# The second product of the attention's scores, contracted over 128 rows instead of 64 or 66

## The chip, the cores and the metric

The kernel runs on one core of a Trainium2 chip. The metric is the device time in microseconds of one execution; the median of three runs is 3224.2 us (3222.32 to 3228.08).

The engines of a core work side by side and wait for each other through semaphores. TensorE (PE in the profile; its weight loads stand apart as PEld) multiplies: one operand of up to 128 x 128 is loaded, the other streams past it column by column, and the rows of both are what the product contracts over. VectorE (DVE) and ScalarE (ACT) work on tiles of up to 128 partitions, GpSimd (POOL) has little to do in this kernel, and SyncE (SP) issues most transfers. The results of TensorE lie in PSUM, eight banks of 128 x 512 float32.

## The reference

One inference step of a two-layer backbone for 128 context tokens and 512 latent tokens of width 1024. Each layer has a half-step feed-forward, three gated mixers side by side (a gated DeltaNet, a grouped-query attention, a linear recurrence) and another feed-forward, all in float32. The attention of the latent tokens, on which the change bears, reads 128 cached context keys and 512 latent keys in one softmax:

```python
def blocked_attention(q, k, v):
    ...
    def one_block(qblk):
        s = jnp.einsum('bqkgd,bskd->bkgqs', qblk, k, preferred_element_type=jnp.float32) * scale
        p = jax.nn.softmax(s, axis=-1).astype(v.dtype)
        return jnp.einsum('bkgqs,bskd->bqkgd', p, v)
```

There are 8 query heads and 2 key heads of width 64, so head `j` and head `j + 4` (for `j` from 0 to 3) belong to the two key heads.

## The kernel before

Tokens stand in columns (640 of them, the context first), features on the 128 partitions; a half of the tokens has 320 columns. TensorE multiplies in a rounded form of float32 (`fp32r`), and each float32 operand is split into a rounded part and the rest (`wh` and `wl` of a weight; `t_H` and `t_A` of the activations), so that a product with weights is three matmuls. The layers follow each other; in a layer the first feed-forward, the mixers, the merge and the second feed-forward. Instructions are emitted in the order of the Python code, with generators that lay steps of one part beside another (`beside`), and a scheduling layer then places them on each engine's queue. Every engine takes its queue in order.

The scores of the attention are split in the same way. For a key head `g`, `kk[g]` holds the rounded keys twice, in both halves of the partitions, and a query operand `q1` holds the rounded queries in one half and their remainder in the other: one product over 128 rows gives two of the three terms. The third term, rounded queries (`q2`, rows 0 to 63) with the remainder of the keys (`kl[g]`, rows 0 to 63), is a second product into the same bank. The scores are computed twice:

- `att_max` (L990): for a pair of heads, query tiles of 128 against halves of 320 keys, only to find each query's maximum. 16 pairs of products for each `j` (2 heads, 4 query tiles, 2 halves), each followed by a maximum on VectorE (L1010). The minus maximum, in two parts, is then written into rows 64 and 65 of `q2`, where `kl[g]` has ones. These are the products `acc<-t_A,t_H` of the profile: 128 x 320 the first, 64 x 320 the second.
- `att_pv` (L1027): key tiles of 128 against all 512 queries, transposed; the second product contracts over 66 rows and so subtracts the maximum. Then the exponential on ScalarE and the products with the values. These are `acc<-t_H,t_A`, 128 x 512 and 66 x 512.

`att` (L1076) runs `att_max(0)` alone, and then, beside the key tiles of each `att_pv(j)`, two steps of `att_max(j + 1)`; a step is two pairs. `beside` lays parts of the merge (`tg`, `wacc<-t_A,wh`) between. Both operands of a head lie in one slot of class H (8 buffers, tile `t_H`); PSUM has five banks for `acc`, of which `att_pv` keeps two for a whole `j`, and three for `wacc`.

The line numbers of helpers, not of the callers, stand in the profile: L174 is every matmul, L154 every ScalarE instruction, L157, L161 and L165 most of VectorE's.

Of the kernel before, what the change touches and what calls it, by code (L numbers as in the profile page):

```python
# [18 lines left out]
P = 128  # L19
# [13 lines left out]
# inverse square root: the seed's bits, the two constants of the first step, the factor left to whoever reads it  # L33
# [14 lines left out]
def spread(n, a, b):  # L48
    """n things over the steps a to b: how many beside each step"""
    return lambda i: (min(max(i + 1 - a, 0), b - a) * n) // (b - a) - (min(max(i - a, 0), b - a) * n) // (b - a)  # L50


# vectors of the next layer's modulation done beside a layer's last feed-forward
MOD2 = 3
# the steps of a feed-forward that its feature tiles lie beside: the first layer's first one, a layer's last, the next's first
STEPS1, STEPS2, STEPS3 = (4, 66), (10, 66), (4, 66)
# tiles over which the first half runs ahead: the first of a feed-forward, its last ones, the last of the mixers
HEAD, TAIL, TAIL_O = 2, 2, 3
# buffers of split weights
WB = 7  # L60
# key tiles whose probabilities are not split
PVF = (0, 2)
# PSUM banks kept for products with weights
WBANKS = 3
# order of the halves of the tokens: that without context tokens is the sooner normed
HO = (1, 0)
# gate tiles emitted behind each projection of the DeltaNet; those left for the attention
FILL = ((1, 1, 0, 1, 1, 1), 4)
# steps emitted behind each step of the DeltaNet's solve, its back part, the attention, the attention's front
# [3 lines left out]
class Slots:  # L73
    """SBUF slots of a few sizes, shared by all that fits them"""
# [28 lines left out]
class Trunk:  # L103
# [24 lines left out]
    # ------------------------------------------------------------- helpers  # L128
# [7 lines left out]
    def late(s, out, in_):  # L136
        """a load that does not run ahead of what precedes it on the scalar queue"""
        s.tc.keep_in_program_order(s.nc.scalar.dma_start(out=out, in_=in_))

    def pairs(s, n):  # L140
        """n views of [P, T], two to a slot; and the slots"""
        regs = [s.A(2 * T) for _ in range(n // 2)]
        return [regs[i // 2].v(2)[:, i % 2, :] for i in range(n)], regs
# [44 lines left out]
    # ------------------------------------------------------------- weights  # L188
    def prep(s, src, nk, m=P):
        """(hi, lo) of weights, four tiles of rows at a time"""  # L190
        nc = s.nc
        parts = []
        for k0 in range(0, nk, WK):
            n = min(WK, nk - k0)
            w = s.wp.tile([P, WK, P], F32, name="w", tag="w", bufs=3)
            wh = s.wp.tile([P, WK, P], F32R, name="wh", tag="wh", bufs=WB)
            wl = s.wp.tile([P, WK, P], F32R, name="wl", tag="wl", bufs=WB)
            nc.sync.dma_start(out=w[:, :n, :m], in_=src[:, k0:k0 + n, :])
            s.act(wh[:, :n, :m], w[:, :n, :m])
            s.tt(wl[:, :n, :m], w[:, :n, :m], wh[:, :n, :m].bitcast(F32), ALU.subtract)  # L200
            parts.append((wh, wl))
        return parts
# [31 lines left out]
    # ------------------------------------------------------------- modulation  # L234
# [25 lines left out]
    def start(s, mc):  # L260
        """the first norm, with the two modulation vectors that it takes"""
# [44 lines left out]
    def mod_cols(s, mc, j, f, pin=False):  # L306
        """feature tile f of modulation vector j; pin: not ahead of what precedes it on the vector engine"""
        nc = s.nc
        l, m = mc["l"], mc["m"]
        cs = s.cs  # L310
        q = j * KT + f
        w = s.wm[q % 2]
        nc.sync.dma_start(out=w, in_=s.a["wmod"][l, q])
        i = s.stt(s.jk.ap, w, 0.5, cs[:, 0, :], ALU.mult, ALU.mult, accum_out=m[:, 0, q:q + 1])
        if pin:
            s.tc.keep_in_program_order(i)
        s.stt(w, w, 0.5, cs[:, 1, :], ALU.mult, ALU.mult, accum_out=m[:, 1, q:q + 1])
# [16 lines left out]
    def mod_steps(s, n):  # L334
        """n more feature tiles of the modulation under way"""
# [10 lines left out]
    # ------------------------------------------------------------- norms  # L346
    def rstd(s, v, out):
        """RS * out = v ** -0.5: a seed from the bits, a quadratic and a cubic step"""
# [54 lines left out]
    # ------------------------------------------------------------- feed-forward  # L403
    @staticmethod
    def halves(n, first, last):
        """(tile, half) with the first half ahead over the first `first` and the last `last` tiles"""
# [5 lines left out]
    def ffn(s, wgu, wd, i, mods, done):  # L412
        """mods(step): feature tiles of a modulation to emit beside; done(o, h): after the last update of a tile's half"""
# [37 lines left out]
    # ------------------------------------------------------------- mixers: shared pieces  # L451
    PADW = 646

    def conv_in(s, w):
        """a projection in padded columns; steps: each half"""
# [12 lines left out]
    def conv(s, xp, taps, bias=None):  # L468
        """centred depthwise convolution of width 4"""
# [11 lines left out]
    def head_rstd(s, xs, scale):  # L481
        """RS * r = (scale * (sum of squares over each 64 rows) + EPS) ** -0.5 for xs of [P, T], heads on partitions;
        returns what spreads r over the rows again: (tile, half) -> [P, H] in PSUM"""
# [21 lines left out]
    def log1p(s, e, n):  # L505
        """log(1 + e), 0 <= e <= 1, for small [P, n]; returns a region"""
# [13 lines left out]
    # ------------------------------------------------------------- gated DeltaNet  # L520
    def dn_front(s):
# [3 lines left out]
        # gates per token: beta and the log decay  # L525
# [3 lines left out]
        # k, q, v: convolution, silu, l2 norm  # L529
# [28 lines left out]
        # token-major k and v; k k^T and k q^T within chunks  # L558
# [33 lines left out]
    def dn_gates(s, baf):  # L592
        """beta, the log decays' running sums and what comes of them"""
# [21 lines left out]
        # running sums within a chunk, per direction; columns (t, d, h)  # L615
# [11 lines left out]
        # rows of gc, spread over the partitions by way of DRAM  # L627
# [22 lines left out]
    def dn_solve(s):  # L650
        """minus the inverses of the diagonal blocks of 32, one system to a partition"""
# [34 lines left out]
    def dn_join(s):  # L686
        """the blocks off the diagonal: minus the inverses of the 64 x 64 systems, transposed, in place"""
# [32 lines left out]
    def dn_back(s):  # L720
        """chunk by chunk, the directions side by side; rows of keys are (chunk of the token tile, dk)"""
# [22 lines left out]
        for i in range(NT):  # L744
            for d in range(2):
# [44 lines left out]
                # states; that ahead of a tile's first chunk is set by the tile before, but for the two starts  # L790
# [32 lines left out]
    def dn_gate(s):  # L823
        """2 silu(z), parked"""
# [11 lines left out]
    def dn_out(s):  # L836
        """per-head norm and silu(z) gate; leaves (hi, lo) of the branch's output"""
# [15 lines left out]
    # ------------------------------------------------------------- attention  # L853
    def att_front(s):
# [40 lines left out]
        # values, token-major  # L895
# [22 lines left out]
        # [v0 | 1 | v1 | low part of v0 | 0 | low part of v1] per key tile: the cache, then the latents  # L918
# [5 lines left out]
        # whole, for the key tiles that take float32 products  # L924
# [15 lines left out]
        for g in range(2):  # L940
# [6 lines left out]
            s.act(s.kl[g][64:66, :], s.ones[64:66, 0:1].to_broadcast([2, T]))  # L947
# [42 lines left out]
    def att_max(s, j, qs):  # L990
        """operands and row maxima for heads j and j + 4, into qs; a step: 128 queries of one head"""
# [3 lines left out]
        for g in range(2):  # L995
# [3 lines left out]
            q1, q2 = reg.r[:, :TL], reg.r[:, TL:2 * TL]  # L999
            s.act(q1[r], src)  # L1000
            s.act(q2[0:64], src)
            s.tt(q1[ro], src, q1[r].bitcast(F32), ALU.subtract)
            for qt in range(4):
                c = slice(qt * P, qt * P + P)
                for h in range(2):
                    ps = s.bank()
                    s.mm(ps[:, :H], q1[:, c], s.kk[g][:, s.hs(h)], True, False)
                    s.mm(ps[:, :H], q2[0:64, c], s.kl[g][0:64, s.hs(h)], False, True)
# [4 lines left out]
        # rows 64 and 65 of the second operand: minus the maximum, in two parts  # L1013
# [13 lines left out]
    def att_pv(s, j, qs):  # L1027
# [4 lines left out]
        for kt in range(NT):  # L1032
            pr = []
            c = slice(kt * P, kt * P + P)
            for g in range(2):
                st = s.bank()
                s.mm(st, s.kk[g][:, c], qs[g][1], True, False)
                s.mm(st, s.kl[g][0:66, c], qs[g][2][0:66], False, True)
# [62 lines left out]
    # ------------------------------------------------------------- RG-LRU  # L1101
    def lru(s):
# [5 lines left out]
        # kappa / 4 = -2 softplus(-lam)  # L1108
# [15 lines left out]
        for j in range(2):  # L1124
# [11 lines left out]
            for d in range(2):  # L1136
# [7 lines left out]
                # tau = tanh(log_a / 2); a = (1 + tau) / (1 - tau); sqrt(1 - a^2) = 2 sqrt(-tau) / (1 - tau)  # L1144
                s.act(y, tr, AF.Exp, scale=small.ap[:, 12 + i4:13 + i4], bias=small.ap[:, 12 + i4:13 + i4])
                s.act(tr, tr, AF.Tanh, scale=kq[:, i4:i4 + 1], bias=kq[:, i4:i4 + 1])
                # 1 / (1 - tau) = (1 + a) / 2; a Newton step
# [21 lines left out]
            # gelu (tanh form) of the y projection  # L1169
# [19 lines left out]
    # ------------------------------------------------------------- merge  # L1189
# [4 lines left out]
    def gates(s, n):  # L1194
        """tanh of half the gates' logits for n more of their tiles, parked"""
# [25 lines left out]
    @staticmethod  # L1221
    def beside(main, fill, n):
        """main's steps, with n[i % len(n)] steps of fill behind step i"""
        for i, _ in enumerate(main):
            for _ in range(n[i % len(n)]):
                next(fill, None)

    @staticmethod
    def both(*gs):
        """steps of several, in turn"""  # L1230
# [8 lines left out]
    def merge_first(s):  # L1239
        """the DeltaNet's and the RG-LRU's part of the merge"""  # L1240
# [66 lines left out]
    # ------------------------------------------------------------- the whole  # L1307
# [9 lines left out]
    def ahead_mix(s, l):  # L1317
        """the first weights of the mixers, ahead of the norm"""
        return lambda: [s.prep(s.a["wba"][l], KT, 16), s.prep(s.a["win"][l, 0], KT)]

    def ahead_ffn(s, wgu):
        """the first weights of a feed-forward"""
# [51 lines left out]
def _layout(i):  # L1374
# [11 lines left out]
    # columns of w_in by tile  # L1386
# [11 lines left out]
    # small parameters per partition  # L1398
# [17 lines left out]
    # (layer, direction, dk, head, dv)  # L1416
# [8 lines left out]
    # constants of the shapes  # L1425
# [51 lines left out]
```

## Time and profile before

| | before |
|---|---|
| timed runs, median (lowest to highest) | 3224.2 us (3222.32 to 3228.08) |
| profiled execution, its span (the page gives no other time of it) | 3222.9 us |
| what lies between the span and the median of the runs | 1.3 us |
| TensorE busy with matmuls, share of the span | 99% |
| VectorE, ScalarE, GpSimd busy | 61%, 36%, 0% |
| mean granted clock of TensorE | 0.990 |

The span is one profiled execution, from its first instruction to its last. "Busy" of an engine counts instructions under way, and since matmuls overlap, a busy TensorE isn't a TensorE at its peak; what a matmul costs is seen in the distance of one start from the next. "Idle before" of a group is the time in which the engine stood still just before its instructions, with what ended it; "issue" there means that nothing the profile shows was waited for.

### The profile page before, as it was taken

To read this page: it belongs to the slowest core of one execution; us is meant where nothing else is said; L and a number is where in the kernel's file an instruction comes from. 1 tells how busy PE (TensorE), PEld (TensorE's weight loads), DVE (VectorE), ACT (ScalarE), POOL (GpSimd) and SP (SyncE) were. 2 spreads that over 40 slices of the span, in tenths; PEclk is the share of its full clock that TensorE was granted. 3 is DMA by queue.
4 is the path that set the end of the run, shared out by engine and by line. 5 is a ranking of instruction groups with operands and counts; after the bars stand their busy time and mean duration, and the time that the engine had idled before them with its cause. 6 is when DMAs were issued, how large, how long until landed. Compare 5 with 4: busy or idle time off the path is not lost.

```text
span 3222.9 us, 54120 instructions
## 1 busy us (share of the span) xinstructions
PE 3176.3 (99%) x21446; PEld 2978.3 (92%) x21446; DVE 1981.2 (61%) x4040; ACT 1159.8 (36%) x2288; POOL 3.8 (0%) x6
## 2 busy tenths in 40 slices
PE   8999999999999999999999999999999999999999
PEld 5999998998976899999999999989889669999999
DVE  5677677667656774555566666685685576633332
ACT  4222324346434443222233222253563343432221
POOL 0000000000000000000000000000000000000000
PEclk9999999999989999999999999999999899999999
DMA  5444442454311422333324444434532124222222
GB/s 218 134 147 168 144 155 89 134 163 119 111 56 54 136 84 99 113 117 99 115 76 138 141 148 133 130 103 144 162 112 81 49 64 140 73 77 77 76 71 81
DMA packets 261466, 364.87 MB, mean 113 GB/s; under 512 B 97708, under 2 KB 144636, under 8 KB 260476
## 3 DMA queue, kind: packets, MB, share of 16 engines
q1 hardware_dynamic: 252572, 340.66, 33.6%
q10 hardware_dynamic: 8640, 20.76, 1.8%
q8 instruction: 168, 2.75, 0.3%
q14 instruction: 86, 0.70, 0.1%
HBM read 325.37 MB, written 35.96 MB: 112 GB/s over the span
## 4 chain that ended last, share of the span: by engine, by line
PE 92%; DVE 4%; ACT 2%; DMA 1%; issue 1%; SPq 1%; ACTq 0%; DVEq 0%
PE wacc L174 49%; PE acc L174 43%; ACT t_A L154 1%; DVE tn L165 1%; DVE t_H L165 1%; SPq L696 0%; DVE wl L157 0%; DMA w<-in_wgu 0%; ACT t_W L154 0%; ACT t_B L154 0%; DVE t_A L157 0%; DVE t L165 0%; DVE t_A L165 0%; DMA gd<-tg 0%; ACT t_H L154 0%
## 5 line engine op out<-in xcount | busy, mean ns | idle before, releaser
L174 PE MATMUL wacc<-t_H,wh 128*128 128x320 f32 (+1 forms) x5568 | 1259.7, 312 | 18.7 <-ACT t_H L154 8.5
L174 PEld LDWEIGHTS wacc<-t_H,wh 128*128 128x128 f32 (+1 forms) x5568 | 932.3, 188 | 42.6 <-ACT t_H L154 11.8
L174 PE MATMUL wacc<-t_H,wl 128*128 128x320 f32 (+1 forms) x2784 | 863.4, 311 | 2.3 <-DVE wl L157 2.3
L154 ACT ACTIVATE wh<-w 128x512 fp32r<-128x512 f32 (+2 forms) x796 | 485.7, 612 | 848.1 <-PE wacc L174 626.3
L157 DVE TENSOR_TENSOR wl<-w,wh 128x512 fp32r<-128x512 f32 (+2 forms) x796 | 527.8, 665 | 329.0 <-ACT wh L154 322.0
L174 PE MATMUL acc<-t_H,wh 128*128 128x320 f32 x2816 | 626.3, 308 | 0.0
L174 PEld LDWEIGHTS wacc<-t_H,wl 128*128 128x128 f32 (+1 forms) x2784 | 522.6, 188 | 11.1 <-issue 5.6
L174 PE MATMUL wacc<-t_A,wh 128*128 128x320 f32 x2048 | 471.8, 313 | 5.3 <-DVE tg L165 4.4
L174 PEld LDWEIGHTS acc<-t_H,wh 128*128 128x128 f32 x2816 | 471.7, 188 | 0.8 <-ACT wh L154 0.2
L174 PE MATMUL acc<-t_H,wl 128*128 128x320 f32 x1408 | 433.3, 308 | 0.4 <-DVE wl L157 0.4
L174 PE MATMUL acc<-t_A,wh 128*128 128x320 f32 x1792 | 397.1, 308 | 0.0
L174 PEld LDWEIGHTS wacc<-t_A,wh 128*128 128x128 f32 x2048 | 345.7, 188 | 18.3 <-issue 7.5
L174 PE MATMUL wacc<-t_A,wl 128*128 128x320 f32 x1024 | 319.7, 312 | 0.0
L174 PEld LDWEIGHTS acc<-t_A,wh 128*128 128x128 f32 x1792 | 299.7, 187 | 0.5 <-ACT t_A L154 0.5
L174 PE MATMUL acc<-t_A,wl 128*128 128x320 f32 x896 | 275.8, 308 | 0.0
L174 PEld LDWEIGHTS acc<-t_H,wl 128*128 128x128 f32 x1408 | 264.0, 188 | 0.7 <-DVE wl L157 0.7
L157 DVE TENSOR_TENSOR th<-th,acc 128x320 f32<-128x320 f32 x176 | 85.6, 488 | 249.4 <-PE acc L174 249.4
L174 PEld LDWEIGHTS wacc<-t_A,wl 128*128 128x128 f32 x1024 | 192.8, 188 | 6.2 <-issue 4.6
L154 ACT ACTIVATE t_A<-th 128x320 fp32r<-128x320 f32 x176 | 82.8, 471 | 295.6 <-DVE th L157 294.7
L174 PEld LDWEIGHTS acc<-t_A,wl 128*128 128x128 f32 x896 | 168.0, 187 | 0.0
L165 DVE SCALAR_TENSOR_TENSOR t_W<-t_W 128x1024 f32<-128x1024 f32 x128 | 156.3, 1221 | 2.2
L165 DVE SCALAR_TENSOR_TENSOR t_A<-acc,mG,t_A 128x320 f32<-128x320 f32 x80 | 44.0, 550 | 182.8 <-PE acc L174 175.0
(180 smaller groups left out, 2761.2 us busy)
## 6 DMA issues: line engine op xcount, KB each, us to landing
w<-in_wgu SPq DMA_DIRECT2D x352, 256.0 KB, 2.8
t_W<-in_wmod SPq DMA_DIRECT2D x128, 512.0 KB, 4.0
w<-in_win SPq DMA_DIRECT2D x168, 256.0 KB, 2.9
w<-in_wd SPq DMA_DIRECT2D x128, 256.0 KB, 2.7
gd<-tg SPq DMA_DIRECT2D x96, 160.0 KB, 2.4
tg<-gd SPq DMA_DIRECT2D x96, 160.0 KB, 2.3
w<-in_wd SPq DMA_DIRECT2D x64, 192.0 KB, 2.4
t_A<-in_wmod SPq DMA_DIRECT2D x16, 512.0 KB, 7.7
```

Source lines behind the costliest of these rows:

```text
L154: return s.nc.scalar.activation(out=out, in_=in_, func=func, **kw)
L157: return s.nc.vector.tensor_tensor(out=out, in0=a, in1=b, op=op)
L165: return s.nc.vector.scalar_tensor_tensor(out=out, in0=a, scalar=sc, in1=b, op0=op0, op1=op1, **kw)
L174: s.nc.tensor.matmul(out, lhsT, rhs, start=start, stop=stop)
```

## The change

The second product of the scores contracts over all 128 rows in both places. For that, rows 64 to 127 of `q2` are set to zero by GpSimd before it is filled (rows 64 and 65 then receive the maxima as before), and rows 64 to 127 of `kl[g]` are all ones, where 64 and 65 were. All other hunks of the diff only take comments out; they move line numbers by at most one from L1000 on.

```diff
@@ att_front
-            s.act(s.kl[g][64:66, :], s.ones[64:66, 0:1].to_broadcast([2, T]))
+            s.act(s.kl[g][64:128, :], s.ones[64:128, 0:1].to_broadcast([64, T]))
@@ att_max
             q1, q2 = reg.r[:, :TL], reg.r[:, TL:2 * TL]
+            nc.gpsimd.memset(reg.ap[64:128, TL:2 * TL], 0.0)
             s.act(q1[r], src)
             s.act(q2[0:64], src)
...
                     s.mm(ps[:, :H], q1[:, c], s.kk[g][:, s.hs(h)], True, False)
-                    s.mm(ps[:, :H], q2[0:64, c], s.kl[g][0:64, s.hs(h)], False, True)
+                    s.mm(ps[:, :H], q2[:, c], s.kl[g][:, s.hs(h)], False, True)
@@ att_pv
                 s.mm(st, s.kk[g][:, c], qs[g][1], True, False)
-                s.mm(st, s.kl[g][0:66, c], qs[g][2][0:66], False, True)
+                s.mm(st, s.kl[g][:, c], qs[g][2], False, True)
```

No instruction changes its place on TensorE, VectorE, ScalarE or the queues. GpSimd's whole program after its start is this now, with what each instruction waits for (`t_W` is a tile of the DeltaNet's solve, `t_H` the slot of a head's two operands):

```order
L663 MEMSET t_W 32x2048 [waits DMAHW3_49,DVE_49]
L1000 MEMSET t_H 64x512 [waits DVE_49,PE_49] x3
L1000 MEMSET t_H 64x512 [waits PE_49]
L1000 MEMSET t_H 64x512 [waits DVE_49,PE_49,Pool_49]
L1000 MEMSET t_H 64x512 [waits DVE_49,PE_49]
L1000 MEMSET t_H 64x512 [waits PE_49,Pool_49]
L1000 MEMSET t_H 64x512 [waits DVE_49,PE_49]
L663 MEMSET t_W 32x2048 [waits DMAHW3_49,DMAHW2_49,DMAHW4_49,DMAHW1_49,DMAHW6_49,DMAHW0_49,DVE_49]
```

Eight memsets of layer 0 stand between the two that were there; eight more follow for layer 1. They wait for what last used their buffer.

On TensorE the pairs of `att_max(0)` in layer 0, before (-) and now (+): the first two heads, whose operands are in `t_H`.

```order
 L174 MATMUL acc<-t_B 64x512 [waits Activation_49]
-L174 MATMUL acc<-t_A,t_H 128x320 x2
+L174 MATMUL acc<-t_A,t_H 128x320
+L174 MATMUL acc<-t_A,t_H 128x320 [waits Pool_49]
 L174 MATMUL acc<-t_A,t_H 128x320 [waits PE_49]
 L174 MATMUL acc<-t_A,t_H 128x320 x3
```

The order is the same; the first second product of a head now also waits for that head's memset, 16 such places in all.

## Rows read from the trace of the kernel before

**Rows 1.** The page: busy time by engine, and the chain's shares.

```profile
PE 3176.3 (99%) x21446; PEld 2978.3 (92%) x21446; DVE 1981.2 (61%) x4040; ACT 1159.8 (36%) x2288; POOL 3.8 (0%) x6
...
PE 92%; DVE 4%; ACT 2%; DMA 1%; issue 1%; SPq 1%; ACTq 0%; DVEq 0%
```

**Rows 2.** Groups by shape: count | busy us, mean ns | idle before, and its enders.

```profile
L1010 DVE TENSOR_REDUCE t_S<-acc 128x1 f32<-128x320 f32 x128 | 62.6, 491 | 54.5 <-PE acc L174 54.4
...
L174 PEld LDWEIGHTS acc<-t_A,t_H 64*128 64x128 f32 x128 | 25.3, 198 | 28.6 <-issue 28.6
...
L154 ACT ACTIVATE t_H<-t_A 64x512 fp32r<-64x512 f32 x32 | 19.1, 623 | 0.3
...
L174 PEld LDWEIGHTS acc<-t_H,t_A 66*128 66x128 f32 x80 | 15.2, 190 | 2.6 <-issue 1.0
...
L157 DVE TENSOR_TENSOR t_H<-t_A,t_H 64x512 fp32r<-64x512 f32 x16 | 11.0, 686 | 17.3 <-ACT t_H L154 17.1
...
L663 POOL MEMSET t_W<- 32x2048 f32 x2 | 3.6, 1800 | 2059.5 <-DMA w<-in_wd 1585.4 <-DVE t_W L165 474.1
```

**Rows 3.** Weight loads in time order: start us, duration us, instruction [idle before].

```profile
976.62 0.19 PEld L174 LDWEIGHTS acc<-t_A,t_H 128*128 128x128 f32 x1
977.00 0.18 PEld L174 LDWEIGHTS acc<-t_A,t_H 64*128 64x128 f32 x1 [0.19 <-issue]
977.35 0.98 PEld L174 LDWEIGHTS acc<-t_H,t_A 128*128 128x128 f32 x5 [0.16 <-ACT t_H L154]
...
984.04 0.19 PEld L174 LDWEIGHTS acc<-t_A,t_H 128*128 128x128 f32 x1 [0.16 <-issue]
984.38 0.18 PEld L174 LDWEIGHTS acc<-t_A,t_H 64*128 64x128 f32 x1 [0.15 <-issue]
984.72 0.19 PEld L174 LDWEIGHTS acc<-t_A,t_H 128*128 128x128 f32 x1 [0.15 <-issue]
```

**Rows 4.** Stretches: length, busy (count) by engine, granted clock, DMA share, GB/s.

```profile
943.90:947.70 3.80, 3.80 (x13) 2.08 (x12) 2.27 (x5) 0.79 (x4) 0.00 (x0) 1.00 0.00 0
947.70:961.90 14.20, 13.64 (x29) 7.43 (x28) 5.63 (x13) 0.00 (x0) 0.00 (x0) 0.50 0.00 0
961.90:968.20 6.30, 5.40 (x21) 3.32 (x22) 2.59 (x8) 1.38 (x3) 0.00 (x0) 0.50 0.41 118
968.20:1060.00 91.80, 91.79 (x383) 60.55 (x383) 63.90 (x121) 40.01 (x78) 0.00 (x0) 1.00 0.18 56
...
2529.00:2534.90 5.90, 5.90 (x19) 3.25 (x18) 3.75 (x8) 0.79 (x4) 0.00 (x0) 1.00 0.01 3
2534.90:2547.10 12.20, 10.74 (x23) 5.91 (x22) 5.40 (x14) 0.21 (x1) 0.00 (x0) 0.50 0.01 1
2547.10:2552.00 4.90, 4.90 (x21) 3.10 (x21) 1.38 (x3) 1.18 (x2) 0.00 (x0) 0.50 0.50 157
2552.00:2644.00 92.00, 91.99 (x384) 60.78 (x383) 63.89 (x121) 40.25 (x79) 0.00 (x0) 1.00 0.18 56
...
1400.00:1420.00 20.00, 20.00 (x139) 20.00 (x138) 10.45 (x20) 6.12 (x11) 0.00 (x0) 1.00 0.38 127
```

**Rows 5.** The first such stretch of layer 0, in time order, loads, maxima, products.

```profile
943.89 0.19 PEld L174 LDWEIGHTS acc<-t_A,t_H 128*128 128x128 f32 x1 [0.81 <-issue]
...
944.68 0.49 DVE L1010 TENSOR_REDUCE t_S<-acc 128x1 f32<-128x320 f32 x1 [2.23 <-PE acc L174]
...
961.38 0.49 DVE L1010 TENSOR_REDUCE t_S<-acc 128x1 f32<-128x320 f32 x1 [0.64 <-PE acc L174]
...
963.37 3.58 PE L174 MATMUL acc<-cst,t_S 128*2 128x128 f32 x16
966.87 1.22 PE L174 MATMUL acc<-t_H,t_A 128*128 128x512 f32 x2
```

**Rows 6.** Waits from 968.2 to 1060: us in total, times, longest.

```profile
DVE t_S L1010 <- PE acc L174: 16.4, 41, 1.0
PEld acc L174 <- issue: 16.0, 79, 0.4
```

## The prediction

> **What bounds the kernel now.** I read the page first. TensorE (PE) is busy for 99% of the span and carries 92% of the chain that ended last [rows 1], so time comes out only where PE steps get shorter or its waits go. Nearly all its work is products with weights, which the change leaves alone; it touches the attention's scores. So I went to the groups by shape. The second product of a pair in `att_max` (64 rows of contraction, 320 columns, 128 of them in the program) has a peculiarity: before its weight load the load side of PE stood idle 28.6 us in all, 0.22 us each, with no engine named as the cause ("issue"). The product with 66 rows in `att_pv` has 2.6 us over 80, next to nothing [rows 2].
>
> The rows in order of time show what that idle time is. In a run of such pairs the loads start 0.34 us apart, alternately 128 and 64 rows: each waits until the product before it has streamed, and only then loads (0.18 to 0.19 us) [rows 3]. In a stretch of products with weights at the same full clock, all 128 rows high, PE does 139 products of 320 columns in 20.00 us, 0.144 us each, and the load side is busy all the time: there the next load lies under the running product (from 1400 to 1420 us) [rows 4]. So a 64-row product costs twice: its own load can't lie beside the 128-row product ahead of it, nor the next 128-row load beside it.
>
> Next I asked for the stretches of the attention. In each layer there are two kinds. In the first (A: 943.9 to 968.2 us in layer 0, 2529.0 to 2552.0 in layer 1) the 16 pairs of the first two heads run almost alone, and part way the granted clock falls from 1.00 to 0.50, which of its two levels (2.4 and 1.2 GHz) is the lower one, and stays there to the end of the stretch. In the second (B: 968.2 to 1060, and 2552 to 2644) the other 48 pairs lie among the exponentials, the products with values and the merge of another branch; the clock is 1.00, and VectorE (DVE) is busy 63.9 of 91.8 us [rows 4].
>
> **The change part by part.**
>
> *Products in A.* Before, the first load is at 943.89 and the stretch at the low clock ends at about 968.2: 24.3 us, and 23.0 us in layer 1. A pair of 128-row products takes 2 x 0.144 = 0.29 us of PE. Then the row maxima are late next: DVE needs 0.49 us for each [rows 2], so 16 x 0.49 = 7.8 us, and some 0.6 us until the first can start. (That these run one behind the other without a wait for PE is my reading; before, they waited for PE each time.) Behind the last maximum, from its end at 961.88 to 968.2, lie 6.3 us: the small work on the maxima, 16 short products from 963.37 to 966.87 (3.5 us), and 1.3 us of the next products [rows 5], all at the low clock. If PE's work is closed up I expect the clock to stay at 1.00, since the low clock began behind a run of pairs 0.68 us long each and rose behind the closed-up 16 short products; these 4.8 us are then 2.4, and the 6.3 become 3.9. Sum: 0.6 + 7.8 + 3.9 = 12.3 us in place of 24.3 and 23.0: 12.0 + 10.7 = 22.7 us saved.
>
> *Products in B.* A pair that stands alone saves at most 2 x (0.34 - 0.144) = 0.39 us. Where the 128-row load came early, the pair took from 976.76 (its first product starts about 0.14 behind the load of 976.62) to 977.35 [rows 3], 0.59 us, and saves 0.30. So PE can give back 48 x 0.30 = 14.4 to 48 x 0.39 = 18.8 us a layer. But where pairs follow each other DVE's 0.49 us sets the pace, and then only 0.68 - 0.49 = 0.19 us a pair is left, 9.1 us. DVE has the room on average: 63.9 busy us in 91.8 - 16 = 76 is 84%, and 16.4 us of its idle time is its wait for just these products [rows 6]. But it won't have room in every place. I take 12 us a layer, between the two, 24 us in both.
>
> *Products with 66 rows.* Their loads hardly waited before [rows 2]: they already went as 128-row loads go, and the 512 columns stay. Nothing gained or lost in 80 products.
>
> *Sixteen memsets on GpSimd (64 x 512), one ahead of each head's operand.* No such shape is in the trace. The nearest row is a memset of 32 x 2048 at 1.80 us [rows 2]; by columns a quarter, 0.45 us, at most those 1.8. GpSimd has nothing else to do there. The memset waits for the same buffer as ScalarE's first copy, and the second product that needs it also needs two copies of 0.62 us and a subtraction of 0.69 us [rows 2], 1.9 us: it is hidden by them, just so at 1.8. Behind the waiting product PE's whole queue stands, so what isn't hidden counts in full. If a memset kept DVE from its memory for its time, 16 x 0.45 = 7 us would be the price, and below zero it can't be. I take nothing and keep 7 for the range. The Trainium skill (SBUF — State Buffer, Who interferes with whom) says that a vector instruction with two SBUF inputs is held only by a GpSimd instruction that reads SBUF, and a memset only writes; by that the price is nothing too, and no run so far shows it.
>
> *The rest.* Ones into 64 rows in place of 2: the same 640 columns on ScalarE, four times, nothing. ScalarE's write of the two rows of maxima now waits for the memset, long done by then. The order on PE, DVE, ScalarE and the queues stays.
>
> Sum: 22.7 + 24 = 46.7 us off the profiled execution's 3222.9 us, which is 1.3 us under the median of the timed runs (3224.2), so 3177.5, say **3178 us**.
>
> **Rivals.**
> *The clock falls in A all the same* (chance 0.22). For it: DVE now paces the pairs, so PE still pauses, and the clock fell in both layers at the same place. Then some seven maxima are done by 947.7, the other nine pairs take 0.58 us (twice 0.29) and seven products with weights between them 0.29 each: 7.2 us, to 954.9, and the 6.3 us behind them stay: 961.2 in place of 968.2. If the low clock lasts as long as before, the first 7 us of B give half of that back. 3.5 to 7 us a layer, 5.2 in the middle, and 24 in B: 34 us off, 3190.
>
> *DVE sets the pace nearly everywhere in B* (0.10): reciprocals and differences queue ahead of the maxima, and B gives 4 us a layer: 22.7 + 8, so 3193.
>
> *DVE doesn't bind* (0.15): B gives 16 us a layer, 22.7 + 32 = 54.7: 3169.
>
> *No gain* (0.03). The wait could belong to any load behind a product on the same rows; then 128 rows load no earlier, and the time stays at 3224. Against it are the 139 products in 20.00 us with loads beside them [rows 4], all on 128 rows. The Trainium skill has that rule: TensorE: Matmul & The Clock Gate, in Measured speedup vs the span model, says that loads overlap running products only when their row groups differ. By that rule the pairs would stay as they are, at 3224; here the trace contradicts it, at 0.144 us a product with a load of 0.19.
>
> *Slower* (0.02): the low clock holds through B. PE, waiting more often for DVE, would have it at 0.50 as in A; its work in B, which I put at 70 us (91.8 less the 16 of the products and some 6 of other waits), would take 140 where 91.8 stood, 48 us lost a layer less some 11 won in A: 75 us, about 3299. It decides once about 46 us of a layer's B run at the low clock, since each costs half a microsecond. Against it: through B the clock is 1.00 in both layers with the load side busy for only 61 of 92 us [rows 4].
>
> **How the numbers follow.** My forecast has 0.48. The range takes it, "DVE doesn't bind" and its upper end of 18.8 us a layer on one side (22.7 + 37.6 = 60 off, 3164), and on the other the clock's fall, the slow B and up to 7 us for memsets (3190 + 7 = 3197): 3164 to 3197. Differences under 0.2% (6 us) can't be told from none. Faster: 0.48 + 0.22 + 0.10 + 0.15 = 0.95; same 0.03; slower 0.02.
>
> **What would show it.** In the profile after: no idle "issue" time ahead of the second product's load, and steps near 0.144 us in a pair; the stretch from the first pair to the end of the 16 short products about 11 us, with the clock at 1.00 (or, by the first rival, at 0.50 for part of it); B near 80 us; DVE's wait for these products down from 16.4 us; memsets near 0.45 us and no wait for GpSimd on PE. I am wrong if the loads still wait (no gain), if A shrinks by less than 8 us a layer, or if B keeps more than 88 of its 92 us.

## The result, and the profile after

| | before | after |
|---|---|---|
| timed runs, median (lowest to highest) | 3224.57 us (3222.32 to 3228.08) | 3167.28 us (3165.95 to 3172.92) |
| ratio of the two, 95% interval | 1 | 0.9824 [0.9812, 0.9835] |
| profiled execution, its span | 3222.9 us | 3171.1 us |
| mean granted clock of TensorE | 0.990 | 0.995 |

Before has four runs here; the three of the first table are among them. The change saves 57 us; 3178 was forecast, with 3164 to 3197 as the range. The profiled execution of after is the longest of its four runs (3172.92 us), so the two traces differ by 51.8 us only; of the other 5 us no trace tells where they lie.

The page of after, busy time and the chain's shares:

```profile
PE 3121.1 (98%) x21446; PEld 2968.1 (94%) x21446; DVE 1975.0 (62%) x4040; ACT 1160.1 (37%) x2288; POOL 12.1 (0%) x22
...
PE 90%; DVE 5%; ACT 3%; issue 1%; DMA 1%; DVEq 0%; ACTq 0%
```

Against [rows 1] TensorE is still the bound, with 55 us less busy time over the same 21446 products: no product went, they stand closer.

The groups that answer to [rows 2], by shape: count | busy us, mean ns | idle before, and its enders.

```profile
L1011 DVE TENSOR_REDUCE t_S<-acc 128x1 f32<-128x320 f32 x128 | 55.6, 485 | 11.4 <-PE acc L174 10.6
L174 PEld LDWEIGHTS acc<-t_A,t_H 128*128 128x128 f32 x256 | 41.9, 188 | 12.1 <-DVE t_H L157 2.7 <-DVE t_S L1011 2.2 <-issue 2.1
L1000 POOL MEMSET t_H<- 64x512 f32 x16 | 8.2, 521 | 1066.0 <-PE wacc L174 909.1 <-PE acc L174 125.3 <-issue 31.6
```

Ahead of the second product's loads stood 28.6 us of "issue" [rows 2]; now the loads of both products together have 2.1. VectorE's wait for these products fell from 54.4 to 10.6 us. A memset takes 0.52 us.

Weight loads in time order, first the pairs of the first heads, then a piece of the stretch behind them (start, duration, instruction, [idle before]):

```profile
944.83 2.35 PEld L174 LDWEIGHTS acc<-t_A,t_H 128*128 128x128 f32 x16 [0.81 <-issue]
947.14 0.19 PEld L174 LDWEIGHTS wacc<-t_A,wl 128*128 128x128 f32 x1
947.29 0.33 PEld L174 LDWEIGHTS acc<-t_A,t_H 128*128 128x128 f32 x2
...
959.95 0.30 PEld L174 LDWEIGHTS acc<-t_A,t_H 128*128 128x128 f32 x2
960.21 0.19 PEld L174 LDWEIGHTS wacc<-t_A,wl 128*128 128x128 f32 x1
960.36 0.80 PEld L174 LDWEIGHTS acc<-t_H,t_A 128*128 128x128 f32 x4
961.20 0.42 PEld L174 LDWEIGHTS acc<-t_A,t_H 128*128 128x128 f32 x2
```

Sixteen loads take 2.35 us, 0.144 us from one to the next, where [rows 3] showed 0.34. Behind the first, none waits for "issue".

VectorE over the same pairs:

```profile
945.43 6.46 DVE L1011 TENSOR_REDUCE t_S<-acc 128x1 f32<-128x320 f32 x16 [2.48 <-PE acc L174]
951.81 0.48 DVE L157 TENSOR_TENSOR t_A<-tg 128x320 f32<-128x320 f32 x1
```

All sixteen maxima run without a gap, and VectorE is what the stretch waits for. But they take 6.46 us, 0.40 each from start to start: one lasts 0.485 us, and the next starts before it has ended.

The stretches that answer to [rows 4] (length, busy and count by engine, granted clock, DMA share, GB/s): A and B of layer 0, A in two parts and B of layer 1, and the stretch of products with weights:

```profile
944.80:955.90 11.10, 9.09 (x62) 7.99 (x62) 9.04 (x24) 2.17 (x7) 0.00 (x0) 1.00 0.13 41
955.90:1032.30 76.40, 75.78 (x382) 58.38 (x382) 62.12 (x122) 40.04 (x78) 2.60 (x5) 1.00 0.23 71
...
2502.40:2510.40 8.00, 6.01 (x40) 5.72 (x39) 7.37 (x21) 0.99 (x5) 0.00 (x0) 1.00 0.01 2
2510.40:2513.40 3.00, 2.98 (x21) 2.17 (x22) 1.60 (x5) 1.18 (x2) 0.00 (x0) 1.00 0.49 153
2513.40:2591.20 77.80, 76.06 (x384) 58.68 (x383) 62.15 (x122) 40.21 (x78) 2.60 (x5) 1.00 0.22 70
...
1372.60:1392.60 20.00, 20.00 (x139) 20.00 (x138) 10.45 (x20) 6.12 (x11) 0.00 (x0) 1.00 0.37 126
```

A went from 24.3 and 23.0 us to 11.1 and 11.0, at the clock's upper level throughout. B went from 91.8 and 92.0 to 76.4 and 77.8. The products with weights go as before, 139 in 20.00 us. Since the order on TensorE is the same, the n-th product of one trace can be set against the n-th of the other: after starts the first pair 0.94 us later than before, is 12.48 ahead behind A (13.4 won), 27.77 behind B (15.3), and in layer 1 12.0 and 14.2 are added. A gave 25.4 us and B 29.5.

Waits in B of layer 0, against [rows 6] (us in total, times, longest):

```profile
DVE t_S L1011 <- PE acc L174: 3.2, 7, 0.8
PEld acc L174 <- issue: 2.2, 10, 0.2
PEld acc L174 <- DVE t_S L1011: 0.4, 2, 0.2
```

16.4 us of VectorE's waiting became 3.2, and 16.0 us of late loads 2.2. Loads hardly wait for a maximum to give back its bank: 0.4 us.

### The profile page after: what moved, and what is told of

Its sections match the earlier page's. It is cut to its first block, busy times and chain, and to the rows that moved or that the text cites. A ratio compares the mean times of both kernels' runs of the same rounds, so it can differ in the third digit from the quotient of the medians.

```text
span 3171.1 us, 54192 instructions
## 1 busy us (share of the span) xinstructions
PE 3121.1 (98%) x21446; PEld 2968.1 (94%) x21446; DVE 1975.0 (62%) x4040; ACT 1160.1 (37%) x2288; POOL 12.1 (0%) x22
## 4 chain that ended last, share of the span: by engine, by line
PE 90%; DVE 5%; ACT 3%; issue 1%; DMA 1%; DVEq 0%; ACTq 0%
PE wacc L174 49%; PE acc L174 40%; ACT t_A L154 1%; DVE tn L165 1%; DVE t_H L165 1%; DVE t_A L157 1%; DVE t_S L1011 1%; DVE wl L157 0%; ACT t_H L154 0%; DMA tg<-gd 0%; DMA w<-in_wgu 0%; ACT t_W L154 0%; DVE t L165 0%; ACT t_B L154 0%; DVE tg L165 0%
```

## The experiments

The theory: a load is late only where the number of rows that it and the product before it contract over changes between 64 and 128. That is all of the gain; of the two kinds of product only those of `att_max` matter; and in A the clock stays up because the pauses go. The rivals: 64 rows are slow as such; the memsets or the products with values bear part of it; VectorE or the clock decides. Ratios are to the runs of before on the same chip, whose medians were 3226.25 to 3226.96 us. The first six kernels keep after's order on TensorE (one turns pairs round), VectorE and ScalarE; the last three don't.

**Only the products of the maxima.** After, but the products with values keep their 66 rows.

```diff
-                s.mm(st, s.kl[g][:, c], qs[g][2], False, True)
+                s.mm(st, s.kl[g][0:66, c], qs[g][2][0:66], False, True)
```

> Only the product for the maxima is 128 rows high; the one in the value part keeps its 66 rows; memsets and ones as in the changed kernel. If the gain comes from loads that had to wait behind the 64-row products, all of it is here: 3167 us, within 4 us of the changed kernel. If the 66-row products gained too (80 of them, up to 0.39 us each if each had two late loads, 31 us), it would stay near 3190 to 3198.

Measured: 3170.84 us, 0.9824 [0.981, 0.9837]. The whole gain comes from these 128 products.

**Only the products with values.** The memsets and the ones are as in after, and the maxima keep 64 rows.

```diff
-                    s.mm(ps[:, :H], q2[:, c], s.kl[g][:, s.hs(h)], False, True)
+                    s.mm(ps[:, :H], q2[0:64, c], s.kl[g][0:64, s.hs(h)], False, True)
```

> Only the product in the value part is 128 rows high; the one for the maxima keeps its 64 rows; memsets and ones as in the changed kernel. My theory: no gain, and the memsets are hidden: 3224 us, within 4 us of the kernel before. If the 66-row products were part of the gain: 3195 to 3215. If the memsets cost anything (16 of 0.52 us): up to 8 us slower, 3232.

Measured: 3228.58 us against 3226.96 of before on the same chip, 1.0 [0.9991, 1.0009]. The memsets cost nothing that can be measured, and 128 rows in place of 66 bring nothing. Two loads of this run in time order, and the stretch in which the clock is down:

```profile
976.54 0.19 PEld L174 LDWEIGHTS acc<-t_A,t_H 128*128 128x128 f32 x1
976.91 0.18 PEld L174 LDWEIGHTS acc<-t_A,t_H 64*128 64x128 f32 x1 [0.19 <-issue]
```

```profile
947.90:968.40 20.50, 19.04 (x50) 11.02 (x50) 8.03 (x19) 1.38 (x3) 0.00 (x0) 0.50 0.13 39
```

The late load and the low clock of before are both back.

**66 rows for the maxima.** Everything else as before, with a memset of the two rows more.

```diff
+            nc.gpsimd.memset(reg.ap[64:66, TL:2 * TL], 0.0)
...
-                    s.mm(ps[:, :H], q2[0:64, c], s.kl[g][0:64, s.hs(h)], False, True)
+                    s.mm(ps[:, :H], q2[0:66, c], s.kl[g][0:66, s.hs(h)], False, True)
```

> The kernel before with 66 rows in the product for the maxima too (rows 64 and 65 set to zero by a memset of 2 x 512, and already ones in the keys): two rows more than 64. If anything over 64 rows loads as 128 do: the whole gain, 3167 us, within 4 us of the changed kernel. If the delay goes down with the rows that are missing to 128: about 1 or 2 us of 57 won, 3222.

Measured: 3172.02 us, 0.9828 [0.9814, 0.9841]: the whole gain with two rows. Its groups:

```profile
L174 PEld LDWEIGHTS acc<-t_A,t_H 66*128 66x128 f32 x128 | 24.2, 189 | 1.4
...
L1000 POOL MEMSET t_H<- 2x512 f32 x16 | 8.2, 520 | 1071.5 <-PE wacc L174 913.7 <-PE acc L174 88.3 <-DVE t_S L1011 69.5
```

A load of 66 rows stood idle 1.4 us over 128, one of 64 rows 28.6 [rows 2]. So the step lies between 64 and 66 rows, and the delay doesn't grow with the rows that are missing to 128. The Trainium skill (TensorEngine Tiling (Array Packing), Tiling Modes) lists 64 rows and 128 rows as different tilings, and under Key Properties says that a change of the mode drains TensorE. No trace records the mode; the times here fit that sentence, with a step of 0.34 us in place of 0.144 at each change between 64 and 128 rows.

**Fewer changes of height.** Before, but in every second pair the 64-row product comes first, so that in the code the heights run 128, 64, 64, 128.

```diff
+                    if h == 0:
+                        s.mm(ps[:, :H], q1[:, c], s.kk[g][:, s.hs(h)], True, False)
+                        s.mm(ps[:, :H], q2[0:64, c], s.kl[g][0:64, s.hs(h)], False, True)
+                    else:
+                        s.mm(ps[:, :H], q2[0:64, c], s.kl[g][0:64, s.hs(h)], True, False)
+                        s.mm(ps[:, :H], q1[:, c], s.kk[g][:, s.hs(h)], False, True)
```

> The kernel before, its second product still 64 rows high, but in every other pair the 64-row product goes first, so that heights follow as 128, 64, 64, 128: half as many changes of height for the same products. If a load is late only where the height changes: two pairs take 2 x 0.34 + 2 x 0.15 = 0.98 us in place of 1.36, half of the loads' delay is gone, and 20 to 32 us of the 57 are won: 3192 to 3204. If a 64-row load is late whatever stands ahead of it: three late steps of four, 1.17 us for two pairs, 10 to 16 us won: 3208 to 3214. If only the pair's own height counts: 3224.

Measured: 3207.43 us, 0.9937 [0.9924, 0.9949], 20 us. That lies outside 3192 to 3204 and just beside the second theory's 3208 to 3214, so the time doesn't decide between them; the trace does. In the first pairs, loads in time order:

```profile
944.61 0.29 PEld L174 LDWEIGHTS acc<-t_A,t_H 64*128 64x128 f32 x2 [0.15 <-issue]
945.10 0.30 PEld L174 LDWEIGHTS acc<-t_A,t_H 128*128 128x128 f32 x2 [0.19 <-issue]
945.59 0.29 PEld L174 LDWEIGHTS acc<-t_A,t_H 64*128 64x128 f32 x2 [0.19 <-issue]
946.07 0.30 PEld L174 LDWEIGHTS acc<-t_A,t_H 128*128 128x128 f32 x2 [0.19 <-issue]
```

Two loads of one height take 0.29 us together, the second under the first's product, and only the change waits, 0.19 us. Two 64-row products in a row are as quick as two of 128 rows. That separates the theory from "64 rows are slow": 0.49 us for a load that changes and one that doesn't, 0.34 + 0.15.

My expectation was off because the changes of height were not halved. On TensorE's queue other products stand between most pairs: only 28 of the 128 loads of 64 rows follow another one directly, so 200 of the 256 changes are left. In B of layer 0 there are 9 of 48, and 9 x 0.39 is 3.5 us; set against before product by product, B won 2.9 and 3.1 us. A won more, 7.1 and 8.3 us. There 5 of 16 loads make some 2 us, and the rest I put down to the clock: it fell only at 955.2 in layer 0 (947.7 before [rows 4]) and not at all in layer 1.

**Only the first heads, only the others.** After, with 128 rows in the one set of heads and 64 in the other.

```diff
-                    s.mm(ps[:, :H], q2[:, c], s.kl[g][:, s.hs(h)], False, True)
+                    n = P if j == 0 else 64
+                    s.mm(ps[:, :H], q2[0:n, c], s.kl[g][0:n, s.hs(h)], False, True)
```

The other kernel has `n = 64 if j == 0 else P`; in both the products with values keep 66 rows.

> 128 rows only in the first pair of heads of each layer (32 of the 128 pairs, the two stretches in which the clock fell); the others keep 64 rows. By the traces the changed kernel won 13.4 and 12.0 us there: 25 us, so 3199 us (3195 to 3204), with the clock at 1.00 in both stretches. If a pair is worth the same everywhere, a quarter of 57: 14 us, 3210.

> 128 rows only in the other three pairs of heads (96 of the 128 pairs); the first keeps 64 rows. By the traces 15.3 and 14.2 us were won there: 29 us, so 3195 us (3191 to 3200), with the clock at 0.50 for 17 to 20 us in the first stretch of each layer as before. If a pair is worth the same everywhere, three quarters of 57: 43 us, 3181.

Measured: 3200.93 us, 0.9919 [0.9905, 0.9932], and 3195.02 us, 0.9904 [0.989, 0.9917]: 26 and 32 us, 58 together, all of the change's gain. A and B of layer 0 in the first, and below in the second:

```profile
942.40:953.50 11.10, 9.10 (x62) 8.00 (x62) 9.07 (x24) 2.17 (x7) 0.00 (x0) 1.00 0.13 41
953.50:1045.20 91.70, 91.69 (x382) 60.43 (x381) 63.88 (x122) 39.99 (x78) 2.60 (x5) 1.00 0.19 59
```

```profile
941.60:966.10 24.50, 23.04 (x62) 13.15 (x62) 10.52 (x24) 2.17 (x7) 0.00 (x0) 0.59 0.11 32
966.10:1042.50 76.40, 75.79 (x382) 58.48 (x381) 62.06 (x121) 39.99 (x78) 2.60 (x5) 1.00 0.22 67
```

Each stretch has its length of after where its products have 128 rows and its length of before where they have 64. The two gains don't touch each other: nothing that A wins is given back in B.

**Maxima taken twice.** After, with each maximum taken a second time into the same place: in the one kernel those of the later heads (B), in the other those of the first heads (A, `j == 0`).

```diff
+                    if j > 0:
+                        nc.vector.tensor_reduce(out=nm2.ap[:, i:i + 1], in_=ps[:, :H], axis=AX.X, op=ALU.max)
```

> The changed kernel, each maximum of the last three pairs of heads taken twice by VectorE: 48 more of 0.40 us a layer, 19 us. If TensorE sets the pace there and VectorE has room (62 busy of 76.4 us in the changed kernel), the first 14 us are taken up and 5 to 10 us a layer are lost: 3177 to 3187. If VectorE already sets it, all 19 us: 3205. If the scores' order keeps VectorE's queue off the path altogether: 3167.

> The changed kernel, each maximum of the first pair of heads taken twice: VectorE's pace there is 0.80 us a pair in place of 0.40, slower than the 0.68 us of the kernel before at the full clock, while TensorE's products stay closed up at 128 rows. 16 x 0.40 = 6.4 us a layer are lost in any case: 3180 us. If what dropped the clock before was TensorE's pauses, it drops here too and TensorE's small products behind it cost 2 to 6 us more a layer: 3184 to 3192. If it was the 64-row products themselves, the clock stays at 1.00: 3180.

Measured: 3210.09 us, 0.9948 [0.9935, 0.996], and 3185.48 us, 0.9874 [0.9861, 0.9888]. Here the scheduling layer also laid TensorE's products in another order (794 and 718 of the 21446 places hold another kind of product than in after, nearly all in the attention), so neither is the one edit alone. The first lost some 40 us of the gain by the ratios and 37 by the traces, 19 to 20 a layer, where 48 maxima of 0.40 us make 19. My expectation that VectorE's idle time would take most of them in was wrong. Its B of layer 0, and who waits there:

```profile
954.23:1047.65 93.42, 82.07 (x383) 57.44 (x382) 79.89 (x168) 43.67 (x83) 2.60 (x5) 1.00 0.16 50
```

```profile
PEld acc L174 <- DVE t_S L1013: 11.9, 15, 1.0
...
PE acc L174 <- DVE t_S L1013: 7.1, 14, 0.8
```

Loads wait 11.9 us and products 7.1 us (partly the same time) for the second maximum to give back a bank; in after such waits came to 0.4. TensorE stood still for 11.4 of the 93.42 us, 0.6 of 76.40 in after. How much of the loss the other order brought isn't known. The second kernel lost 18 us (16 by the ratios). Two stretches in A, and two waits from 943.1 to 962:

```profile
943.10:951.80 8.70, 6.61 (x36) 5.17 (x36) 8.10 (x21) 0.79 (x4) 0.00 (x0) 1.00 0.00 0
951.80:962.00 10.20, 6.35 (x24) 3.66 (x23) 7.36 (x20) 1.11 (x3) 0.00 (x0) 0.50 0.17 51
```

```profile
PEld acc L174 <- DVE t_S L1013: 3.8, 5, 0.9
...
PE acc L174 <- DVE t_S L1013: 2.4, 5, 0.6
```

The clock fell to its lower level here with 128-row products alone, behind a run in which TensorE paused for VectorE, and likewise in layer 1 (from 2515.1, for 13.7 us). So it doesn't take products of 64 rows to bring it down.

**Maxima over half of the columns.** After, but each maximum reads 160 of 320 columns, and 40 is added to what is found. A softmax cancels whatever is taken off all scores of a query, so its values need not change by this, other than the expectation says.

```diff
-                    nc.vector.tensor_reduce(out=nm2.ap[:, i:i + 1], in_=ps[:, :H], axis=AX.X, op=ALU.max)
+                    nc.vector.tensor_reduce(out=nm2.ap[:, i:i + 1], in_=ps[:, :H // 2], axis=AX.X, op=ALU.max)
...
         s.tt(nm.ap, nm2.ap[:, :8], nm2.ap[:, 8:], ALU.max)
+        s.ts(nm.ap, nm.ap, 40.0, ALU.add)
```

> The changed kernel, but each maximum reads 160 of its 320 columns, and 40 is added to the maximum found: half of the keys are left out of the search, so that the numbers after the softmax differ from the reference's. The scheduling layer lays some neighbours of the pairs differently for it, so only differences above some 5 us count. It asks whether VectorE still sets the pace once the loads no longer wait. If a maximum costs by its columns (0.398 us apart for 320 in the changed kernel), 160 fewer columns take 0.1 to 0.2 us less. Theory 'VectorE sets the pace in both stretches': in A the 16 pairs go at TensorE's 0.29 us instead of 0.398, 1.7 us a layer, and in B 48 maxima give up to 48 x 0.17 = 8 us a layer: 10 to 19 us less than the changed kernel, 3148 to 3157. Rival 'TensorE sets the pace in B, and VectorE only just keeps up': 1.7 us a layer in A and next to nothing in B: 3162 to 3167, not told apart from the changed kernel.

Measured: 3163.97 us, 0.9811 [0.9797, 0.9824], 3 us under after (4 by the ratios), within the interval. TensorE's order differs here too, in 818 places. The time is the rival's. The loads of the first heads, and the group of the maxima:

```profile
942.64 4.69 PEld L174 LDWEIGHTS acc<-t_A,t_H 128*128 128x128 f32 x32 [0.81 <-issue]
```

```profile
L1011 DVE TENSOR_REDUCE t_S<-acc 128x1 f32<-128x160 f32 x128 | 39.8, 323 | 19.6 <-PE acc L174 18.2
```

A maximum takes 0.162 us less, 64 x 0.162 = 10.4 us a layer, 7.8 of them in B. In A the 16 pairs now go at TensorE's own pace (32 loads in 4.69 us), and the 16 short products start 7.03 us behind the first load in place of 8.33: 1.3 us saved. In B VectorE mostly waits longer for TensorE, 18.2 in place of 10.6 us in all; from the traces B is 1.7 and 2.8 us shorter. So in after TensorE sets most of B's pace: less work for VectorE brought little. That more of it cost some 19 us a layer says that VectorE has little room, as far as two kernels with another order on TensorE can show it.

## Why the prediction was right, point by point

- *The loads wait at 64 rows, and only they.* Right: the idle "issue" time of 28.6 us [rows 2] is gone, the gain is the 128 products' alone, and the runs with 66 rows and with fewer changes show that the change of height is the cause. The rival "no gain" fell. The rule behind it, in the Trainium skill (TensorE: Matmul & The Clock Gate, The mechanism, the section ahead of the one that the prediction names), that loads overlap running products only when their row groups differ, disagrees with this trace: sixteen loads on all 128 rows took 2.35 us, each longer (0.19) than its step (0.144).
- *A: 22.7 us forecast, 25.4 by the products.* The mechanism is right, and so are 0.6 us to the first maximum and 3.9 us behind the last one (951.89 to 955.9, 4.0). The mis-sized term is 16 x 0.49 = 7.8 us of maxima: I took the duration of one (491 ns in [rows 2]) as the distance from one to the next. The distance is 0.40, so 6.4 us. These 1.4 us a layer are the whole error: the sum was short by 2.7 us in two layers. The trace of before had the sign of it: behind the last maximum, which starts at 961.38 [rows 5] and lasts 0.49 us, VectorE's next instruction starts 0.41 us later.

```profile
961.79 0.48 DVE L157 TENSOR_TENSOR t_A<-tg 128x320 f32<-128x320 f32 x1
```

- *The clock stays up in A.* Right, in both layers (1.00 throughout). The rival with the fall (3190) rested on VectorE's pacing, and the doubled maxima show its mechanism is real: with TensorE waiting longer for VectorE the clock fell, 10.2 us at 0.50. In after the pairs were through 5.7 us behind their first load (the last product starts at 950.51), with maxima 0.40 us apart. The fall was near all the same. In five kernels (after, "only the products of the maxima", "66 rows", "only the first heads", and the maxima taken twice in the later heads, which leaves A as it is) the products of A follow each other at this pace, and its 16 short products start 8.3 us behind the first pair. That makes ten stretches. In two of them the clock fell at the end, and the short products took 2.74 us (66 rows, layer 0) and 3.19 us (later heads' maxima twice, layer 1) in place of 1.91. The second of these, and then the same place of after:

```profile
2527.02 3.19 PE L174 MATMUL acc<-cst,t_S 128*2 128x128 f32 x16
```

```profile
2510.76 1.91 PE L174 MATMUL acc<-cst,t_S 128*2 128x128 f32 x16
```

So the long fall of before (20.5 us in layer 0 [rows 4]) is in none of the ten, but closed-up work alone doesn't settle the clock at the end of A. What decides there isn't known, and that the profiled run of after shows no fall at all has some luck in it.

- *B: 24 us forecast, 29.5 measured.* This is the step that failed: "where pairs follow each other DVE's 0.49 us sets the pace". The same figure again, and VectorE set little of it. B gave 15.3 and 14.2 us, at the lower end of what I had said that TensorE can give back (14.4 to 18.8, the lower end being 0.30 a pair), near the rival "DVE doesn't bind" (16 a layer, 3169). With VectorE relieved of 7.8 us a layer there, B shrank by 1.7 and 2.8 us only.
- *The average of 84% for VectorE.* I read it as room that is missing in some places only. The doubled maxima say that there is little: VectorE was busy 62.1 of 76.4 us after, and 19 us more cost 19 to 20, though 14 seemed free (with TensorE's order changed, so the figure is rough).
- *Memsets and the rest: nothing.* Right (1.0 [0.9991, 1.0009]). One takes 0.52 us, not 0.45, and one of 2 rows takes as long as one of 64. TensorE waits nowhere for GpSimd.
- *The sum.* 46.7 us were forecast; the traces show 54.9 in the four stretches, and 51.8 over the span: 0.94 us went before the first pair, and the other 2 us between and behind the stretches, up and down by a microsecond. The medians differ by 57. The likeliest case was right for A. For B the rival "DVE doesn't bind" was nearer, to which I gave 0.15; that its sum of 54.7 meets the 54.9 is luck, since it has 2.5 us too much for B and 2.7 too little for A. The forecast's two errors, one figure used twice, went the same way, and the range was wide enough for them.

## What to carry to other kernels

Where short products stand beside full ones, look at the idle time ahead of their weight loads: here a product of 64 rows between products of 128 cost 0.34 us in place of 0.144, and so did the next one, and zeros up to 66 or 128 rows, written by an idle engine, took that away. Where nothing can be padded, put products of one height next to each other in the queue as it is finally laid out, not only in the code: there, turning every second pair round removed 56 of 256 changes. Read an engine's pace from the distance between starts, not from the duration of one instruction.

## What the runs showed of the hardware that was not expected

- Two maxima over 320 columns in PSUM start 0.40 us apart though each lasts 0.485 us in the trace: some 0.08 us of a reduction lies under the next one.
- A GpSimd memset of 2 x 512 took 520 ns, one of 64 x 512 521 ns: between these two the rows don't count.
- A load of 66 rows behaves as one of 128 (0.189 us, no wait); the step between 64 and 66 rows was worth 55 us of this kernel (3226.96 to 3172.02).
- The clock's lower level appeared behind 128-row products alone when TensorE paused for VectorE (0.50 from 951.8 to 962.0), where the pairs took 10.3 us (from 943.10 to the last product at 953.43) in place of 5.7 in after.
- The same products at the same distances ran at either level: the 16 short products behind the pairs took 1.91 us in eight of ten such stretches, 2.74 and 3.19 in the other two.
